# Weight sums made step by step, and the first h quarters loaded into x5's place

## The chip, the cores and the metric

One core of one Trainium2 chip runs the whole program. The metric is the device time of one execution in microseconds (us); the time before is the median of three runs. A profile was taken of one further execution.

## What is computed

One decoder layer on 512 tokens of width 2048, all in float32. Cut to what matters here:

```python
proj = x @ w_in                                        # 2048 -> 4352: q | k | v | B | C | h
attn = sliding_window_gqa(rope(q), rope(k), v, sinks)  # 16 heads of 64, 2 kv heads, window 128
conv = B * causal_depthwise_conv3(C * h)               # 1024 channels
x = layer_norm(ALPHA * x + concat(attn, conv) @ w_out)
u = causal_depthwise_conv3(x @ w_up)                   # 2048 -> 11264
a, g = split(u)
x = layer_norm(ALPHA * x + (silu(a) * g) @ w_down)     # 5632 -> 2048
```

## The kernel before, in words

**Split operands.** TensorE multiplies in fp32r. `split` (L189) cuts a float32 tile into a rounded part (`hi`, a copy on ScalarE, L190) and the rest (`lo`, a subtraction on VectorE, L191), and each product is two or three matmuls (hi by hi, hi by lo, lo by hi).

**Weights.** All weights lie in DRAM as one list `ws` of chunks of 128 x 2048 (1 MB). `dma_to` (L148) loads them in order on SP's queue into `raw` (3 buffers). `split_to` cuts halves of 1024 columns into `whi` and `wlo` (4 buffers each), two halves ahead of the product that uses them.

**The input projection.** `q_panel(0)`: eight halves with 24 matmuls each; here x itself is loaded too (`load_x`, one piece beside each weight chunk) and split. Then four halves for k and v, then eight for the second half of q. `q_evac` applies the rotary factors: two products on VectorE into `wa` and `wb` (two buffers each), and an addition on GpSimd (POOL, L268). Then 48 conv steps (L833 on), each one half of a conv panel in `feat_half` (24 matmuls), with a piece of attention between. Attention begins with `att_q` (L311): a split of q, then transposes on TensorE (L320).

**The output projection and the first normalisation.** `tok_half` steps, again with `half` for the weights; residual rows z are loaded on SP and the gain and bias `gb` on POOL's queue.

**Up product.** Each of 44 column blocks of W_up is done with seven products instead of eight (a Strassen-like scheme). The operands are sums of quarters of x, held in tiles x1 to x7: x1, x2, x4, x7 lie in the four parts of `act`, and x5, x6, x3 in pools of their own. Sums of weight quarters are made by accumulating DMAs on POOL's queue (`w_add`). `product_order` (L58) writes the order out: the last block (43) ends with products 5, 1, (7 and 3 of block 42), 6, 3, (4 of block 42), 7, 2, 4. Results h go to DRAM (`hd`) in groups of four blocks.

**Down product.** Ten column-and-row blocks n, again seven products each, in the order 5, 1, 2, 6, 3, 7, 4. Their h operands are made from quarters of h: `hq_load` (L611) loads four quarters into tiles of the pool `hr`, and `hx` (L617) adds or subtracts on VectorE and splits into a free place from the list `self.free`. Products 5 and 7 need sums of weight quarters that are prepared in DRAM, 20 in all: `w_sum` (L569) copies one chunk from DRAM to DRAM (L577) and then accumulates two half chunks on it (L581), all issued on POOL's queue. Sum 5 of block n is loaded to `wqd` by `d_load` (L583, POOL's queue), sum 7 by `dma_to`.

**What sets the order.** The Tile framework's planner fixes each engine's instruction order from the data dependencies and from its own cost estimates; each engine, and each queue of DMA issues (SP's and POOL's), then executes in that order. An instruction whose inputs and buffer are free may be put far ahead of its place in the source.

The source asks for sums from within the conv loop, one issue step per conv step, and for the h quarters after the last reader of x3:

```python
            self.w_sum(i - 2)                               # conv step i
...
        self.up(20, last)                                   # last = after (43, 3)
        self.d_load(0)
        self.hq_load(0)
```

Of the kernel before, what the change touches and what calls it, by code (L numbers as in the profile page):

```python
# [8 lines left out]
F32 = mybir.dt.float32  # L9
F32R = mybir.dt.float32r  # L10
AF = mybir.ActivationFunctionType
ALU = mybir.AluOpType
AX = mybir.AxisListType

P = 128
S = 512
D = 2048
KT = D // P
# [6 lines left out]
NF = DFF // P  # L25
H = S // 2
# [10 lines left out]
C_OUT = C_CONV + NC_CONV  # L37
# [3 lines left out]
NB = 2 * (NF // 8)  # L41
# [86 lines left out]
class Kernel:  # L128
# [99 lines left out]

    def tok_half(self, j, ks, n, k0, pss, tbs=range(NTB), ahead=2):
        hi, lo = self.half(j, ks, ahead)  # L230
        for k in range(ks):
            kt = k0 + k
            if j == 0 and k == 0:
                ops = ((0, hi), (0, lo), (1, hi))
                for a, (part, ws) in enumerate(ops):
                    for tb in tbs:
                        self.nc.tensor.matmul(pss[tb], self.A(part, 0, slice(tb * P, (tb + 1) * P)), ws[:, 0, :],
                                              start=a == 0, stop=False)
                continue
            for tb in tbs:  # L240
                sl = slice(tb * P, (tb + 1) * P)
                self.mm3(pss[tb][:, :n], self.A(0, kt, sl), self.A(1, kt, sl), hi[:, k, :], lo[:, k, :],
                         kt == 0, kt == KT - 1)
# [322 lines left out]
        c = slice(1024 * h, 1024 * (h + 1))  # L566
        self.nc.gpsimd.dma_start(t[:, c], self.ws_d[C_DOWN + 4 * n + i][:, c], accum_op=ALU.add)

    def w_sum(self, k):  # L569

        s = k // 2 if k % 2 == 0 else (k - 3) // 2
        if not 0 <= s < 2 * NB:
            return
        n, p = s // 2, (5, 7)[s % 2]
        w = lambda i: self.ws_d[C_DOWN + 4 * n + i]
        if k % 2 == 0:
            self.nc.gpsimd.dma_start(self.sums[n, p], w(3))  # L577
        else:
            for h in range(2):
                c = slice(1024 * h, 1024 * (h + 1))  # L580
                self.nc.gpsimd.dma_start(self.sums[n, p][:, c], w(0 if p == 5 else 2)[:, c], accum_op=ALU.add)  # L581

    def d_load(self, n):  # L583

        if n < NB:
            t = self.wq[n] = self.p_qd.tile([P, 2048], F32, name="wqd")
            self.nc.gpsimd.dma_start(t, self.sums[n, 5])

    def down_prep(self, n, p, h):
# [18 lines left out]
        elif h and p in (1, 2, 3, 7):  # L608
            del self.raw[c]

    def hq_load(self, u):  # L611

        for a, t in ((1, 1), (1, 0), (0, 0), (0, 1)):
            tile = self.hq[t, a] = self.p_hr.tile([P, 4, H], F32, name=f"h{t}{a}")
            self.nc.sync.dma_start(tile, self.hd[2 * u + t][:, :, a * H:(a + 1) * H])

    def hx(self, u, p):  # L617

# [129 lines left out]
    def run(self):  # L748
# [28 lines left out]
        ps = self.psum("aux")  # L777
# [56 lines left out]
        for i in range(2 * NC_CONV):  # L834
            j = 2 * C_CONV + i
            q = i % 4
            if q == 0:
                pss = [self.psum("mm") for _ in range(2)]
            hi, lo = self.half(j, 4)
            self.feat_half(hi, lo, q, pss)  # L840
            self.w_sum(i - 2)
            if q == 3:
                self.conv_evac(i // 4, pss)
            for u, off in ((i, 0), (i - 1, 1), (i - 4, 2), (i - 5, 3)):
                if u % 2 == 0 and 0 <= u // 2 < 16:
                    n = u // 2
                    if off == 0:
                        st[n] = self.att_q(*units[n])
                    elif off == 1:
                        st[n] = self.att_scores(*units[n], st[n])  # L850
                    elif off == 2:
                        st[n] = self.att_transpose(*units[n], st[n])
                    else:
                        self.att_values(*units[n], st.pop(n))
# [10 lines left out]
        for k in (slice(0, 2), slice(2, 8)):  # L865
            for tb in range(NTB):
                sl = slice(tb * P, (tb + 1) * P)
                src = self.qm[tb].rearrange("p (k t) -> p k t", t=P)
# [14 lines left out]
        j = 2 * C_OUT  # L883
# [31 lines left out]
        halves = [self.half(j + h, 4, 7 - h) for h in range(4)]  # L915
# [4 lines left out]
        for tb in range(NTB):  # L920
            ps = self.psum("mm")
            sl = slice(tb * P, (tb + 1) * P)
            for kt in range(KT):
                hi, lo = halves[kt // 4]
# [8 lines left out]
        p_x5 = opened("x5", 1, "right")  # L933
        x5 = p_x5.tile([P, KT * H], F32R, name="x5")
# [19 lines left out]
        for tb in (2, 3):  # L954
# [18 lines left out]
        self.up(8, 20)  # L973
        n = len(self.order)
        last = self.order.index((NF - 1, 3)) + 1
        self.up(20, last)
        cm_x3.__exit__(None, None, None)
        cm_x6.__exit__(None, None, None)
        self.p_qd = opened("qd", 2, "right")
        cm_hr, self.p_hr = self.pool("hr", 1, "right")  # L980
        self.hq, self.xd, self.place = {}, {}, {}
        halves = lambda t: [t[:, :KT * P], t[:, KT * P:]]
        self.free = [x for t in (self.act[:, 0, :], x5, self.act[:, 3, :], self.act[:, 1, :], self.act[:, 2, :])
                     for x in halves(t)]
        self.d_load(0)
        self.hq_load(0)
        for i, ps in zip(range(last, n), ((4, 5, 1, 2), (6, 3), (7,), ())):
            self.up(i, i + 1)
            if i == n - 1:
                self.up_conv(NF - 1, 0)  # L990
                self.up_out(NF - 1)
            for p in ps:
                self.hx(0, p)
        for cm, _ in reversed(cm_up):
            cm.__exit__(None, None, None)
        self.z = {}
# [7 lines left out]
        for i, (m, p, h) in enumerate(self.todo[n:]):  # L1004
            self.prepare(n + i + 4)
            u, c = divmod(m, 2)
            ps = self.down_half(m, p, h)
            if not h:
                continue
            self.down_evac(m, p, ps)  # L1010
            if c:
                self.free.append(self.place[u, p])
            if (m, p) == (0, 1):
                self.d_load(1)
            if u + 1 < NB // 2:
                at, q = (1, {3: 4, 7: 5, 4: 1, 11: 2, 12: 6, 16: 3, 13: 7})
                if u == 0:
                    at, q = (3, {4: 4, 11: 5, 12: 1, 16: 2, 13: 6, 17: 3, 14: 7})
                if 10 * c + p == at:
                    self.hq_load(u + 1)  # L1020
                if 10 * c + p in q:
                    self.hx(u + 1, q[10 * c + p])
                continue
            if not c and p == 1:

                places = [self.free.pop(0) for _ in range(2)]
                hs = [x.rearrange("p (f t) -> p f t", f=4) for x in places]
                for t in range(2):
                    raw = self.p_hr.tile([P, 4, H], F32, name=f"h{t}0")
                    tk = slice(t * H, (t + 1) * H)  # L1030
                    nc.sync.dma_start(raw, self.hd[ND - 1][:, :, tk])
                    self.split(hs[0][:, :, tk], hs[1][:, :, tk], raw)
            if (m, p) not in end:
                continue

            k = end.index((m, p))
            if k < 8:
                x1[k] = self.p_hr.tile([P, 4, H], F32, name=("h01", "h11", "h00", "h10")[k % 4])
                x1[k] = x1[k].rearrange("p k t -> p (k t)")
                nc.sync.dma_start(x1[k], zd[k // 2][:, 1024 * (k % 2):1024 * (k % 2 + 1)])  # L1040
            if k >= 2:
                z = self.zc((k - 2) // 2, 1024 * (k % 2), 1024 * (k % 2 + 1))
                nc.vector.scalar_tensor_tensor(z, x1.pop(k - 2), ALPHA, z, op0=ALU.mult, op1=ALU.add)
            if k == 9:
                cm_hr.__exit__(None, None, None)
                p_gb = opened("gb2", 1, "right")
                self.gb = p_gb.tile([P, 2, D], F32, name="gb")
                for a in range(2):
                    nc.gpsimd.dma_start(self.gb[:, a, :], self.lng_d[2 + a].partition_broadcast(P))
# [28 lines left out]
```

## Time and profile before

| what | value |
|---|---|
| runs | 2043.38, 2045.75, 2046.54 us; median 2045.75 |
| the profiled execution | 2044.12 us, of which the span is 2042.3 us |
| mean granted TensorE clock | 0.975 |
| TensorE busy | 1935.0 us (95%) |
| VectorE, ScalarE, POOL busy | 1383.6, 921.3, 308.8 us |
| DMA | 430.19 MB; POOL's queue 174.76 MB, SP's and ScalarE's 252.73 MB |

The span is what lies between the first and the last instruction. In the page's table of 40 slices a slice is 51 us; TensorE's row is below 9 in slices 0, 1 and 3, at the first normalisation (slices 13 and 14), at the change from up to down product (slice 31) and in the last slice. A matmul with 512 columns is shown with 0.39 us, but they overlap: what counts is the distance of their starts.

### The profile page before, as it was taken

What the parts mean: (1) busy time and instruction counts of PE and PEld (TensorE: products, weight loads), DVE (VectorE), ACT (ScalarE), POOL (GpSimd) and SP (SyncE); (2) the same over time, 40 slices, a digit from 0 to 9 for tenths busy, and PEclk for the clock granted to TensorE, in tenths of its full rate; (3) what the DMA queues carried; (4) which work ended last, traced back from release to release, by engine and by line L of the source; (5) the groups of instructions that cost most, each with busy time, mean ns of one, the idle gap of its engine ahead of it and who ended that gap; (6) DMA issues with size and microseconds to landing.
All of it is one profiled execution on the core that took longest, in us unless ns stands there. A gap on an engine that the chain in (4) does not pass through costs nothing. (4 is left out here: it accounts for less than half of the span.)

```text
span 2042.3 us, 26061 instructions
## 1 busy us (share of the span) xinstructions
PE 1935.0 (95%) x9998; PEld 1645.7 (81%) x9998; DVE 1383.6 (68%) x1959; ACT 921.3 (45%) x1403; POOL 308.8 (15%) x361
## 2 busy tenths in 40 slices
PE   7893999999999699999999999999999799999997
PEld 5682888888889588888888888888887588888876
DVE  3332767635334877777777777777777777887887
ACT  2220455433111555555555555555555564454441
POOL 2223000000001511121111111111121001101104
PEclk9896999999999999999999999999999899999999
DMA  9999622154432669999999999999999687877852
GB/s 306 270 295 260 184 78 83 63 165 156 154 103 87 183 155 261 244 261 254 244 262 236 270 254 245 262 242 268 247 249 262 185 235 200 234 225 201 266 193 82
DMA packets 98172, 430.19 MB, mean 211 GB/s; under 512 B 10240, under 2 KB 21536, under 8 KB 72896
## 3 DMA queue, kind: packets, MB, share of 16 engines
q0 software_dynamic: 40928, 174.76, 42.2%
q1 hardware_dynamic: 56544, 252.73, 34.1%
q8 instruction: 78, 1.28, 0.2%
q10 hardware_dynamic: 576, 1.05, 0.1%
q14 instruction: 46, 0.38, 0.1%
HBM read 408.58 MB, written 61.87 MB: 230 GB/s over the span
## 5 line engine op out<-in xcount | busy, mean ns | idle before, releaser
L191 DVE TENSOR_TENSOR wlo<-raw,whi 128x1024 fp32r<-128x1024 f32 (+1 forms) x358 | 437.3, 1223 | 292.8 <-ACT whi L190 292.4
L190 ACT CAST whi<-raw 128x1024 fp32r<-128x1024 f32 (+1 forms) x358 | 373.4, 1045 | 536.3 <-PE mm L222 107.5
L500 PE MATMUL mm<-act,whi 128*128 128x512 f32 x1056 | 379.3, 400 | 8.9 <-DVE act L191 6.7
L502 PE MATMUL mm<-act,wlo 128*128 128x256 f32 x1056 | 297.3, 282 | 0.0
L500 PE MATMUL c<-x,whi 128*128 128x512 f32 x704 | 250.8, 393 | 0.0
L500 PEld LDWEIGHTS mm<-act,whi 128*128 128x128 f32 x1056 | 199.2, 189 | 58.4 <-DVE act L191 7.0
L451 POOL DMA_DIRECT2D wq<-ws x132 | 127.9, 971 | 703.1 <-DVE wlo L191 559.7
L191 DVE TENSOR_TENSOR wlo<-wq,whi 128x1024 fp32r<-128x1024 f32 x132 | 161.3, 1223 | 83.5 <-ACT whi L190 83.3
L502 PEld LDWEIGHTS mm<-act,wlo 128*128 128x128 f32 x1056 | 200.6, 190 | 0.0
L502 PE MATMUL c<-x,wlo 128*128 128x256 f32 x704 | 199.0, 283 | 0.0
L190 ACT CAST whi<-wq 128x1024 fp32r<-128x1024 f32 x132 | 138.5, 1050 | 133.8 <-PE c L500 51.3
L500 PEld LDWEIGHTS c<-x,whi 128*128 128x128 f32 x704 | 132.2, 188 | 30.3
L221 PE MATMUL mm<-act,whi 128*128 128x512 f32 x384 | 152.0, 396 | 0.0
L223 PE MATMUL mm<-act,wlo 128*128 128x512 f32 x384 | 150.4, 392 | 0.0
L222 PE MATMUL mm<-act,whi 128*128 128x512 f32 x384 | 150.1, 391 | 0.0
L221 PE MATMUL mm<-whi,act 128*128 128x512 f32 (+1 forms) x316 | 120.8, 382 | 21.9 <-ACT act L190 20.8
L502 PEld LDWEIGHTS c<-x,wlo 128*128 128x128 f32 x704 | 132.3, 188 | 0.0
L500 PE MATMUL b<-act,whi 128*128 128x512 f32 x352 | 128.5, 404 | 1.5 <-DVE act L191 1.5
L500 PE MATMUL mm<-x,whi 128*128 128x512 f32 x352 | 125.3, 393 | 0.0
L222 PE MATMUL mm<-wlo,act 128*128 128x512 f32 (+1 forms) x316 | 119.6, 378 | 0.3 <-DVE wlo L191 0.3
L223 PE MATMUL mm<-whi,act 128*128 128x512 f32 (+1 forms) x316 | 119.3, 377 | 0.0
L648 PE MATMUL mm<-whi,act 128*128 128x512 f32 x256 | 99.8, 390 | 5.0 <-DVE z L664 3.3
(217 smaller groups left out, 3868.2 us busy)
## 6 DMA issues: line engine op xcount, KB each, us to landing
raw<-ws SPq DMA_DIRECT2D x170, 1024.0 KB, 7.6
wq<-ws POOLq DMA_DIRECT2D x132, 512.0 KB, 9.2
wq<-ws SPq DMA_DIRECT2D x44, 512.0 KB, 8.1
raw<-ws POOLq DMA_DIRECT2D x44, 512.0 KB, 7.2
sum<-ws POOLq DMA_DIRECT2D x40, 512.0 KB, 15.1
wqd<-ws POOLq DMA_DIRECT2D x40, 512.0 KB, 7.2
hd<-ca SPq DMA_DIRECT2D x44, 256.0 KB, 9.6
h<-hd SPq DMA_DIRECT2D x22, 512.0 KB, 5.2
```

The costliest lines, as they stand in the source:

```text
L190: self.nc.scalar.copy(hi, src)
L191: self.nc.vector.tensor_tensor(lo, src, hi.bitcast(F32), op=ALU.subtract)
L221: mm(ps, sh, mh, start=start, stop=False)
L222: mm(ps, sh, ml, start=False, stop=False)
L223: mm(ps, sl, mh, start=False, stop=stop)
L451: self.nc.gpsimd.dma_start(dst, self.ws_d[C_UP + UP_PIECES[2 * f + i]][:, 1024 * j:1024 * (j + 1)], accum_op=ALU.add)
L500: mm(ps, hi[:, sl], x[:, k, :, :].rearrange("p a t -> p (a t)"), start=new and k == 0, stop=False, skip_group_check=not new)
L502: mm(ps[:, :H], lo[:, sl], x[:, k, 0, :], start=False, stop=k == 7, skip_group_check=not new)
L648: mm(ps[b], xh, hi[:, k, :], start=new and h == 0 and k == 0, stop=False, **kw)
```

## The change

Two things are changed. The sums in DRAM: sum s is asked for at conv step 3s, and the last four in the output projection (`tok_half`). A small DMA first copies one element of the step's `wlo` to the sum's place; the chunk copy overwrites it and the accumulations follow, each waiting for the one before. The h quarters: right after product (43, 5), x5's place is taken as a tile of four quarters and `hq_load(0)` loads into it; the operands of the first two blocks go to other places, in another order, and two halves of x5 join the end of the free list. `d_load(1)` is asked for one product earlier, with a ScalarE copy of an element of z (a result of product (0, 5)) into its tile ahead of the load.

```diff
 def tok_half(self, j, ks, n, k0, pss, tbs=range(NTB), ahead=2):
     hi, lo = self.half(j, ks, ahead)
+    if C_OUT <= j // 2:
+        self.w_sum(j - 2 * C_OUT + 48, lo.rearrange("p a b -> p (a b)").bitcast(F32))
...
-def w_sum(self, k):
-    s = k // 2 if k % 2 == 0 else (k - 3) // 2
-    if not 0 <= s < 2 * NB:
+def w_sum(self, k, t):
+    s = k // 3
+    if k % 3 or not 0 <= s < 2 * NB:
         return
     n, p = s // 2, (5, 7)[s % 2]
     w = lambda i: self.ws_d[C_DOWN + 4 * n + i]
-    if k % 2 == 0:
-        self.nc.gpsimd.dma_start(self.sums[n, p], w(3))
-    else:
-        for h in range(2):
-            c = slice(1024 * h, 1024 * (h + 1))
-            self.nc.gpsimd.dma_start(self.sums[n, p][:, c], w(0 if p == 5 else 2)[:, c], accum_op=ALU.add)
+    self.nc.gpsimd.dma_start(self.sums[n, p][0:1, 0:1], t[0:1, 0:1])
+    self.nc.gpsimd.dma_start(self.sums[n, p], w(3))
+    for h in range(2):
+        c = slice(1024 * h, 1024 * (h + 1))
+        self.nc.gpsimd.dma_start(self.sums[n, p][:, c], w(0 if p == 5 else 2)[:, c], accum_op=ALU.add)
-def d_load(self, n):
+def d_load(self, n, after=None):
     if n < NB:
         t = self.wq[n] = self.p_qd.tile([P, 2048], F32, name="wqd")
+        if after is not None:
+            self.nc.scalar.copy(t[:, 0:1], after)
         self.nc.gpsimd.dma_start(t, self.sums[n, 5])
-def hq_load(self, u):
-    for a, t in ((1, 1), (1, 0), (0, 0), (0, 1)):
-        tile = self.hq[t, a] = self.p_hr.tile([P, 4, H], F32, name=f"h{t}{a}")
-        self.nc.sync.dma_start(tile, self.hd[2 * u + t][:, :, a * H:(a + 1) * H])
+def hq_load(self, u, places=None):
+    for q, (a, t) in enumerate(((1, 1), (1, 0), (0, 0), (0, 1))):
+        src = self.hd[2 * u + t][:, :, a * H:(a + 1) * H]
+        ...  # into places[q] where given, else into a tile of hr as before
...
-            self.w_sum(i - 2)
+            self.w_sum(i, lo.rearrange("p a b -> p (a b)").bitcast(F32))
...
     last = self.order.index((NF - 1, 3)) + 1
-    self.up(20, last)
+    k = self.order.index((NF - 1, 5)) + 1
+    self.up(20, k)
+    h0 = p_x5.tile([P, KT * H], F32, name="x5")
+    quarters = h0.rearrange("p (q k t) -> p q k t", q=4, t=H)
+    self.hq_load(0, [quarters[:, q] for q in range(4)])
+    self.up(k, last)
...
-    self.free = [x for t in (self.act[:, 0, :], x5, self.act[:, 3, :], self.act[:, 1, :], self.act[:, 2, :])
+    self.free = [x for t in (self.act[:, 0, :], self.act[:, 3, :], self.act[:, 1, :], self.act[:, 2, :])
                  for x in halves(t)]
     self.d_load(0)
-    self.hq_load(0)
-    for i, ps in zip(range(last, n), ((4, 5, 1, 2), (6, 3), (7,), ())):
+    for i, ps in zip(range(last, n), ((4, 5), (1, 2), (6, 3), (7,))):
         self.up(i, i + 1)
...
+    self.free += halves(p_x5.tile([P, KT * H], F32R, name="x5"))
...
-            if (m, p) == (0, 1):
-                self.d_load(1)
+            if (m, p) == (0, 5):
+                self.d_load(1, self.zc(2, 1024, 1025))
```

## Rows read from the trace of the kernel before

**Rows 1.** Windows: length, busy time (instructions) per engine, granted clock, DMA share, GB/s.

```profile
0.00:84.00 84.00, 60.02 (x200) 43.56 (x201) 25.34 (x35) 21.59 (x30) 16.50 (x32) 0.86 0.97 305
84.00:158.00 74.00, 74.00 (x427) 65.03 (x425) 28.04 (x52) 18.56 (x30) 23.02 (x30) 1.00 0.99 275
158.00:192.00 34.00, 0.79 (x6) 0.57 (x5) 5.88 (x8) 1.04 (x1) 13.44 (x16) 0.53 1.01 257
192.00:496.00 304.00, 304.00 (x1487) 255.00 (x1486) 188.93 (x368) 131.53 (x305) 10.26 (x13) 1.00 0.39 118
...
1580.00:1600.00 20.00, 9.70 (x33) 6.78 (x31) 14.17 (x15) 12.04 (x16) 0.87 (x1) 0.74 0.49 121
1600.00:1620.00 20.00, 15.84 (x57) 12.55 (x58) 16.29 (x17) 9.62 (x13) 1.71 (x2) 0.83 0.88 246
1620.00:1640.00 20.00, 20.00 (x89) 16.52 (x89) 15.31 (x16) 10.26 (x13) 2.27 (x3) 1.00 0.78 218
```

**Rows 2.** Waits, whole run: engine, line, releaser, total us, times, longest us.

```profile
ACT act L190 <- DMA xraw<-xt: 39.6, 9, 10.6
```

**Rows 3.** Groups of TensorE's instructions, 0 to 84 us: busy, mean ns, idle before.

```profile
L221 PE MATMUL mm<-whi,act 128*128 128x512 f32 x60 | 27.6, 461 | 21.9 <-ACT act L190 20.8 <-ACT whi L190 1.1
```

**Rows 4.** Timeline of TensorE: start, duration, line, idle before and releaser.

```profile
6.23 2.07 PE L237 MATMUL mm<-whi,act 128*128 128x512 f32 x4 [0.59 <-ACT whi L190]
...
40.44 0.80 PE L221 MATMUL mm<-whi,act 128*128 128x512 f32 x1 [6.42 <-ACT act L190]
...
191.43 0.75 PE L320 MATMUL aux<-identr,qs 128*128 128x128 f32 x4 [33.21 <-DVE qs L317]
```

**Rows 5.** Timeline of POOL and its DMA issues, 0 to 230 us.

```profile
5.17 1.02 POOL L577 DMA_DIRECT2D sum<-ws  x2
14.14 1.76 POOL L581 DMA_DIRECT2D sum<-ws  x2 [7.96 <-DMA sum<-ws]
...
184.55 2.75 POOL L268 TENSOR_TENSOR qm<-wa,wb 128x512 f32<-128x512 f32 x2
...
220.68 1.64 POOL L581 DMA_DIRECT2D sum<-ws  x2 [8.61 <-DMA sum<-ws]
```

**Rows 6.** Timeline of VectorE, 112 to 200 us.

```profile
186.12 0.69 DVE L263 TENSOR_TENSOR wa<-mm,rope_t 128x512 f32<-128x512 f32 x1 [31.41 <-POOL qm L268]
...
188.65 2.72 DVE L317 TENSOR_TENSOR qs<-qm,qs 128x256 fp32r<-128x256 f32 x1
```

**Rows 7.** VectorE's conv results: count, durations, first and last start.

```profile
L413 DVE TENSOR_TENSOR cmix<-mm,wb x8: 680/688/692, 260.7 to 496.6; 128x512 f32<-128x512 f32 x8
```

**Rows 8.** DMA issues: count, KB each, median us to landing; first 84 to 158 us.

```profile
raw<-ws SPq DMA_DIRECT2D x7, 1024.0 KB, 12.6
...
sum<-ws POOLq DMA_DIRECT2D x40, 512.0 KB, 15.1
out<-z SPq DMA_DIRECT2D x14, 256.0 KB, 2.2
sum<-ws POOLq DMA_DIRECT2D x20, 18.3
```

**Rows 9.** Waits of TensorE, 1570 to 1700 us.

```profile
PE mm L500 <- DVE mt L508: 2.1, 1, 2.1
```

**Rows 10.** Timelines of TensorE, POOL, SP and ScalarE around the change to the down product.

```profile
1552.65 0.28 PE L502 MATMUL c<-x,wlo 128*128 128x256 f32 x1
...
1564.50 1.09 POOL L587 DMA_DIRECT2D wqd<-sum  x2 [6.82 <-PE mm L502]
...
1567.08 8.46 SPq L615 DMA_DIRECT2D h<-hd  x4
...
1573.06 1.05 ACT L190 CAST whi<-wqd 128x1024 fp32r<-128x1024 f32 x1 [4.76 <-DMA wqd<-sum]
...
1584.72 1.04 ACT L190 CAST x<-h 128x1024 fp32r<-128x1024 f32 x1 [3.07 <-DMA h<-hd]
...
1588.60 1.04 ACT L190 CAST x<-h 128x1024 fp32r<-128x1024 f32 x1 [1.89 <-DMA h<-hd]
```

More of the change, by code (lines that the diff above doesn't have):

```diff
@@ L609, in down_prep @@
             del self.raw[c]
-    def hq_load(self, u):
-        for a, t in ((1, 1), (1, 0), (0, 0), (0, 1)):
-            tile = self.hq[t, a] = self.p_hr.tile([P, 4, H], F32, name=f"h{t}{a}")
-            self.nc.sync.dma_start(tile, self.hd[2 * u + t][:, :, a * H:(a + 1) * H])
+    def hq_load(self, u, places=None):
+        for q, (a, t) in enumerate(((1, 1), (1, 0), (0, 0), (0, 1))):
+            src = self.hd[2 * u + t][:, :, a * H:(a + 1) * H]
+            if places is None:
+                tile = self.p_hr.tile([P, 4, H], F32, name=f"h{t}{a}")
+                self.nc.sync.dma_start(tile, src)
+            else:
+                tile = places[q]
+                self.nc.sync.dma_start(tile, src)
+            self.hq[t, a] = tile
     def hx(self, u, p):
@@ L975, in run @@
         last = self.order.index((NF - 1, 3)) + 1
-        self.up(20, last)
+        self.hq, self.xd, self.place = {}, {}, {}
+        k = self.order.index((NF - 1, 5)) + 1
[4 more added lines that the diff above has]
+        self.up(k, last)
         cm_x3.__exit__(None, None, None)
@@ L980, in run @@
         cm_hr, self.p_hr = self.pool("hr", 1, "right")
-        self.hq, self.xd, self.place = {}, {}, {}
         halves = lambda t: [t[:, :KT * P], t[:, KT * P:]]
-        self.free = [x for t in (self.act[:, 0, :], x5, self.act[:, 3, :], self.act[:, 1, :], self.act[:, 2, :])
+        self.free = [x for t in (self.act[:, 0, :], self.act[:, 3, :], self.act[:, 1, :], self.act[:, 2, :])
                      for x in halves(t)]
         self.d_load(0)
-        self.hq_load(0)
-        for i, ps in zip(range(last, n), ((4, 5, 1, 2), (6, 3), (7,), ())):
+        for i, ps in zip(range(last, n), ((4, 5), (1, 2), (6, 3), (7,))):
             self.up(i, i + 1)
```

## The prediction

> **What bounds the kernel now.** I read the page's 40 slices first (TensorE below 9 tenths in few of them), then windows cut at those slices, then the waits of each low window, then the timelines. TensorE is the bound wherever its inputs are there: 74.00 of 74 us busy from 84 to 158 us, 304.00 of 304 through the conv stage [rows 1]. So a gain can only come from its idle stretches, and those touched by the change are three.
>
> The first is the first panel, 0 to 84 us: TensorE waits 20.8 us for x's split [rows 3], ScalarE in turn 39.6 us for x from DRAM [rows 2], while the DMA engines are 97% busy [rows 1]. What fills them are the sums, written in the conv loop but issued from 5.17 us on [rows 5], since nothing holds them back.
>
> The second is the gap of 33.2 us ahead of the first attention transposes [rows 4]. Its chain: TensorE waits for VectorE's split of q, which stands in VectorE's order behind the rotary products; those waited 31.4 us for their buffer [rows 6], which POOL's rotary addition frees; that addition ran at 184.55 us because POOL's queue was standing in the accumulations, each waiting for its copy to land [rows 5].
>
> The third is the change to the down product, 1580 to 1620 us: ScalarE waits for the h quarters, the third and fourth of four, split at 1584.72 and 1588.60 us [rows 10]; the reader is to see that they were issued at 1567.08 us, though x5 had its last reader at 1552.65 us.
>
> **The change, part by part.**
>
> *First panel.* It has 192 matmuls (three groups of 60, of which one is shown [rows 3], and 12 started apart). At full clock 89 take 20 us [rows 1], 0.225 us each, so 43.2 us. The 12 at the start, of which four take 2.07 us [rows 4], cost some 2.5 us more and keep that. From 6.2 us the panel could end at 52 us instead of 84: 32 us lost, made of idle time and of the low clock (mean 0.86 [rows 1]) after each gap. With no sums the loads move only weights and x, 8.4 MB for those 46 us, 183 GB/s; the DMA engines moved 305 GB/s there [rows 1]. A lower end: some gaps at the start, when everything lands at once, stay (7 us). I keep 1.5 us: gain 30.5, range 25 to 32.
>
> *The gap at the conv stage.* The accumulations leave POOL's queue ahead of the rotary additions, except those of sum 0: its marker waits for the split of the first conv half, which is made two halves ahead, thus while q's last panel still runs. Behind the marker stands the copy, behind it the accumulations, and if the planner puts these ahead of the additions, the additions wait for the copy's landing; VectorE's rotary products and the q split wait for them. The first copies landed within 14.14 - 5.17 = 9.0 us, beside other loads [rows 5]; VectorE stood ready for its third rotary product at 186.12 - 31.41 = 154.7 us [rows 6], 3.5 us before TensorE ran out at 191.43 - 33.21 = 158.2 [rows 4], so the additions were due before that. Thus between 0 and 9 us of the 33.2 stay. From the additions to the transposes it was 191.43 - 184.55 = 6.9 us [rows 4, 5], which alone leaves 1 to 2. I take 1.7: gain 31.5, range 24 to 34 (the upper end with the low clock after the gap).
>
> *Where the sums go.* Conv steps take (496.6 - 260.7) / 36 = 6.55 us [rows 7], so a sum comes every 19 us or so and the last fall into the output projection. Moved there: 20 copies and 40 accumulations, plus 20 markers. DMA was 39% busy in the conv stage, its first 38 us still with sums [rows 1]. Cover: the weights are loaded three chunks ahead, and a chunk lasts two steps, 13 us. With sums running without pause a chunk landed in 12.6 us [rows 8], and TensorE missed nothing in that stretch although it used a chunk in about 11 us [rows 1]. So I cost this at 0, bound 0 to 15 us, should the loads be late now and then. A marker reads `wlo`, whose buffer is wanted again four steps (26 us) later. No marker is in the trace; the nearest row, a store of 256 KB, lands in 2.2 us [rows 8], a chunk copy in 18.3 at worst of load. Hidden, 0; below nothing it can't go, as it does no work of before.
>
> *The h quarters.* In 1580 to 1620 us TensorE did 33 + 57 = 90 matmuls, for which it needs 20.2 us at the rate of the window after [rows 1]. Lost 19.8 us, and 2.1 us in a wait just ahead [rows 9]: 21.9 us. Now the four loads can start when product (43, 5) ends at 1552.65, 14.4 us sooner than 1567.08 [rows 10]. On SP's queue they wait for that product; behind them stand stores of h and raw chunks for the down product, which take their turn once it ends. The four took 21.5 us to the last split (1567.08 to 1588.60 [rows 10]) in company of 2 MB of `wqd` and other loads; so all are there by 1574 at the latest, before the last up product ends. d_load(1), which was issued along with d_load(0) at 1564.50 [rows 10], is held back until product (0, 5) is out, which leaves its 1 MB some five products of 5.4 us (24 matmuls) to land in. Its ScalarE copy is one element a row: nothing.
>
> What is late next: VectorE. It was busy 14.17 + 16.29 = 30.5 us in those 40 [rows 1]; if TensorE is to pass through in 20 us, what of this is not done earlier must fit beside it. Only products 4 and 5's operands can move ahead of 1570; products 1, 2, 6, 3 and 7 now take places (x7's, x2's, x4's) that come free with the last three up products, later than x5's half, which served 1 and 2 before. And `wqd` for product (0, 5) still comes at 1573 [rows 10] unless fewer loads run beside it. I keep 6 of the 21.9: gain 16, range -3 (a chain put in a worse order) to 21.
>
> *Sum.* 30.5 + 31.5 + 0 + 16 = 78 us. Everything after each gap is TensorE-bound, so the shifts carry through. The profiled execution took 2044.1 us (its span 2042.3 and 1.8 around it); 2044.1 - 78 = 1966.1. The median is 1.6 above that execution: 1968 us.
>
> **Rivals.**
>
> *The sums hurt where they now run* (slower). If each sum delayed TensorE as it did in the first panel, where some seven sums cost 32 us, 20 sums cost 91 us: 2044 - 78 + 91 + 2 = 2059 us. It decides once a chunk takes over some 25 us to land, twice its use. For it: the first panel itself. Against it: the first panel needed x besides, 1 MB in 5.4 us, twice the conv stage's need or more, and the stretch from 84 to 158 us ran full under the same load [rows 1]. The Trainium skill, in "DMA: Bandwidth & Descriptors", section "Issuing engines are not separate DMA queues", says that DMAs started from different engines run on the same 16 DMA engines and interleave; by that alone the collisions would only move. Trace and rule agree on the collision, in the first panel.
>
> *The marker chain paces TensorE.* Copy and accumulations in series, each as late as before: 2.2 + 18.3 + 15.1 = 35.6 us [rows 8] a sum instead of 19, with `wlo` held: 20 x 16.6 - 26 = 306 us, 2274 us in all. Against it: those landings come from several sums at once; one alone needs the 9 us of the first copies and about as much again, and POOL doesn't wait for the accumulations' end.
>
> *The h part gives nothing.* The planner may put the second set of h loads, which no longer waits for the first's tiles, as far ahead as d_load(1) was, so that they collide with `wqd`; or VectorE stays the limit. Then 1984 us.
>
> *Only half of the conv gap goes*: sum 0's accumulations stand before the additions, and what they delay is a chain of several engines: 15 of 33 us stay, 1981 us.
>
> *The change doesn't do what it says*: the sums' order is still the planner's. But the marker is a data dependency on a split, so no sum can start before it; I give this little. With the first panel alone improved: about 2014 us.
>
> **How the numbers follow.** The forecast as worked out 0.66 (1955 to 1978); h part nothing 0.13; conv gap half 0.08; both of these or the doing-less case 0.05 (1990 to 2020); sums hurt in the conv stage 0.05, of which half ends above the time before; marker chain 0.03. What a measurement can tell from no change is 0.2%, 4 us. Faster: the first four and half of the fifth, 0.94; within 4 us: 0.01; slower: 0.05. Best ends give 2044.1 - 32 - 34 - 21 + 1.6 = 1959; some unlisted gain of the shift may come on top, so low 1954. The high end takes in the two smaller cases: 1995.
>
> **What would show it.** After: first copy on POOL's queue past 100 us; the first panel's end near 53 us with no wait over 2 us; POOL's additions right behind VectorE's products and the transposes' wait under 3 us; raw chunks landing in under 13 us in the conv stage and TensorE full there; h loads issued some 14 us before the last product that reads x3 ends; TensorE's clock at 1.00 through the change to the down product, or else waits there for VectorE. Wrong would be the sum if TensorE shows new waits for `wlo` or raw in the conv stage, or if the additions still stand behind a landing.

## The result, and the profile after

The changed kernel takes 1969.53 us (median of 4 runs, 1967.84 to 1970.89); the kernel before took 2045.31 beside it. The ratio is 0.963, with a 95% interval of 0.9613 to 0.9647. The profiled execution has a span of 1969.1 us, 73.2 less than before, and a mean granted clock of 0.989 against 0.975. The forecast was 1968.

The windows of the changed kernel, cut at the same stages; the columns are those of [rows 1]:

```profile
0.00:52.00 52.00, 50.09 (x203) 38.99 (x204) 25.61 (x36) 21.67 (x30) 5.02 (x16) 1.00 0.65 255
52.00:126.00 74.00, 74.00 (x430) 65.19 (x429) 30.41 (x59) 19.02 (x31) 16.51 (x16) 1.00 0.37 114
126.00:430.00 304.00, 304.00 (x1492) 255.02 (x1492) 190.95 (x370) 132.83 (x306) 45.36 (x65) 1.00 0.74 202
...
1510.00:1520.00 10.00, 8.72 (x35) 7.36 (x36) 9.41 (x14) 8.20 (x13) 1.71 (x2) 0.83 0.90 219
1520.00:1530.00 10.00, 5.00 (x23) 3.79 (x21) 9.99 (x12) 8.13 (x11) 0.56 (x1) 0.97 0.48 151
1530.00:1540.00 10.00, 9.63 (x30) 7.75 (x31) 9.20 (x9) 4.13 (x5) 1.71 (x2) 0.68 0.86 271
```

The reader is to see three things. The first panel, 84 us with a clock of 0.86 before, is done in 52 with a clock of 1.00. No window stands between the end of q, k and v and the conv stage: the 34 us of 158 to 192 are gone. And the conv stage is as full as it was (304.00 of 304), although DMA is now busy for 74% of it and not 39%. At the change to the down product, though, TensorE still loses time, and VectorE is busy 9.2 to 10 us of each 10.

ScalarE's wait for x in the first panel, which was 39.6 us [rows 2], and the loads of x on SP's queue, first of the kernel before, then of the changed one (count, KB each, median us to landing):

```profile
ACT act L190 <- DMA xraw<-xt: 5.0, 6, 2.2
```

```profile
xraw<-xt SPq DMA_DIRECT2D x6, 512.0 KB, 32.4
...
xraw<-xt SPq DMA_DIRECT2D x6, 512.0 KB, 9.6
```

POOL and TensorE where the gap was (timelines; compare [rows 5] and the last row of [rows 4]):

```profile
105.03 0.54 POOL L579 DMA_DIRECT2D sum<-wlo  x1 [24.24 <-DVE wlo L191]
106.92 0.51 POOL L580 DMA_DIRECT2D sum<-ws  x1 [1.34 <-DMA sum<-wlo]
112.16 1.75 POOL L583 DMA_DIRECT2D sum<-ws  x2 [4.74 <-DMA sum<-ws]
119.31 2.56 POOL L270 TENSOR_TENSOR qm<-wa,wb 128x512 f32<-128x512 f32 x2 [5.40 <-DVE wb L268]
```

```profile
125.57 0.45 PE L322 MATMUL aux<-identr,qs 128*128 128x128 f32 x4
```

Sum 0 is begun at 105 us, its two accumulations leave the queue together from 112.16 us on (each waits for the copy, neither for the other), and the rotary additions, at 119.31, wait for VectorE's product and not for a landing. The transposes follow without a wait where 33.2 us stood.

In the conv stage, VectorE's results and the DMA issues of 130 to 430 us (issues: KB each, median us to landing):

```profile
L415 DVE TENSOR_TENSOR cmix<-mm,wb x8: 682/691/692, 193.5 to 429.3; 128x512 f32<-128x512 f32 x8
```

```profile
raw<-ws SPq DMA_DIRECT2D x23, 1024.0 KB, 5.1
sum<-ws POOLq DMA_DIRECT2D x30, 512.0 KB, 8.5
...
sum<-ws POOLq DMA_DIRECT2D x16, 5.1
sum<-wlo POOLq DMA_DIRECT2D x15, 0.0 KB, 4.8
```

The first and the last result come 67.2 us earlier than in [rows 7], so all of this part of the gain is there before the conv stage and nothing is lost in it. A chunk of weights lands in 5.1 us where the sums ran beside it in 12.6 before [rows 8].

The waits of TensorE at the change to the down product, and the timeline there, all engines in one by their start:

```profile
PE mm L660 <- DVE wlo L191: 5.4, 1, 5.4
PE mm L502 <- DVE mt L510: 2.8, 1, 2.8
```

```profile
1485.61 0.28 PE L504 MATMUL c<-x,wlo 128*128 128x256 f32 x1
...
1485.98 4.65 SPq L625 DMA_DIRECT2D x<-hd  x4
...
1497.47 0.55 POOL L592 DMA_DIRECT2D wqd<-sum  x1 [6.45 <-PE mm L504]
...
1507.22 1.05 ACT L190 CAST whi<-wqd 128x1024 fp32r<-128x1024 f32 x1 [4.98 <-DMA wqd<-sum]
...
1522.54 1.22 DVE L630 TENSOR_TENSOR x<-x 128x1024 f32<-128x1024 f32 x1
...
1527.36 1.22 DVE L191 TENSOR_TENSOR act<-x,act 128x1024 fp32r<-128x1024 f32 x1
...
1529.10 3.49 DVE L191 TENSOR_TENSOR wlo<-raw,whi 128x1024 fp32r<-128x1024 f32 x3
...
1530.37 0.79 PE L660 MATMUL mm<-wlo,act 128*128 128x512 f32 x1 [5.38 <-DVE wlo L191]
```

The h loads leave 0.4 us after the last matmul of product (43, 5) starts (14.4 before [rows 10]). But the weight split that TensorE wants at 1525 stands on VectorE behind sums and splits of h operands (the L630 and act rows) that are only needed later.

### The profile page after: what moved, and what is told of

The parts are those of the page before. It is cut to its first block, busy times and chain, and to the rows that moved or that the text cites. A ratio compares the mean times of both kernels' runs of the same rounds, so it can differ in the third digit from the quotient of the medians.

```text
span 1969.1 us, 26106 instructions
## 1 busy us (share of the span) xinstructions
PE 1923.1 (98%) x9998; PEld 1640.4 (83%) x9998; DVE 1380.6 (70%) x1959; ACT 920.8 (47%) x1404; POOL 323.0 (16%) x381
## 5 line engine op out<-in xcount | busy, mean ns | idle before, releaser
L221 PE MATMUL mm<-whi,act 128*128 128x512 f32 (+1 forms) x316 | 116.5, 369 | 0.0
L223 PE MATMUL mm<-whi,act 128*128 128x512 f32 (+1 forms) x316 | 116.2, 368 | 0.0
L660 PE MATMUL mm<-wlo,act 128*128 128x512 f32 x272 | 107.4, 395 | 5.4 <-DVE wlo L191 5.4
```

Source lines behind the costliest of these rows:

```text
L221: mm(ps, sh, mh, start=start, stop=False)
L223: mm(ps, sl, mh, start=False, stop=stop)
L660: mm(ps[b], xh, lo[:, k, :], start=False, stop=False, **kw)
```

## The experiments

**One half at a time.** `sums_only` keeps the sums' part and undoes the h part; `h_only` does the opposite:

```diff
 # sums_only, against the changed kernel
-    h0 = p_x5.tile(...); self.hq_load(0, [quarters[:, q] for q in range(4)])
...
+    self.hq_load(0)                 # after d_load(0); operand order, places, d_load(1) as before
 # h_only: w_sum as before
-    self.nc.gpsimd.dma_start(self.sums[n, p][0:1, 0:1], t[0:1, 0:1])
...
+    self.w_sum(i - 2)
```

> Only the sums are paced by markers; the h quarters and the places are as before. Theory (the sums' part is worth the 67 us by which every stage after the conv gap is earlier in the changed kernel): 2045.3 - 67 = 1978 us, span shift 67 at the end of the up product and still 67 at the end, with the stalls at the change to the down product as before (16.6 us of waits). Rival (the two parts need each other, or part of the 67 belongs to the h part): over 1985 us.

> Only the h quarters' part (early loads into x5's place, other places, d_load(1) held); the sums are asked for as before. Theory from the traces (the h part gains 9.6 us up to product (0, 3) of the down product, and some 3 us are lost again in the last stage): 2045.3 - 6.5 = 2039 us. The prediction's term was 16: 2029 us. Rival (the h part gains nothing by itself): within 4 us of 2045.

`sums_only` took 1976.76 us, ratio 0.9651 (0.9633 to 0.9668), span 1975.0: 67.3 less than before. `h_only` took 2038.05, ratio 0.9945 (0.993 to 0.996): 11.1 less than the 2049.19 of before beside it (8 to 14 by the interval; 6.1 in the spans, 2042.3 - 2036.2). Both came within 1.3 us of their theories. Nearly everything is the sums' part, and the h part is worth less than the 16 us forecast: 11.1 alone, and in the spans 1975.0 - 1969.1 = 5.9 on top of the other (1975.0 - 1966.9 = 8.1 with the second profile of the changed kernel, below). By the ratios 0.9651 and 0.9630, or 0.9620 in the repeat, it is 4 to 6 us, uncertain by some 5.

**The two gaps of the sums' part.** `sums_after_panel` is the kernel before with 20 small copies, one per sum, tied to the third weight half of k and v, so that the sums start only after the first panel, and are unpaced from there on. `rope_vector` is the kernel before with the rotary additions on VectorE:

```diff
 # sums_after_panel, in q_panel
+        if j == 10:
+            self.marks(lo)     # sums[n, p][0:1, 0:1] <- lo[0:1, 0:1], for all 20
 # rope_vector
-        nc.gpsimd.tensor_tensor(dst, t1, t2, op=ALU.add)
+        nc.vector.tensor_tensor(dst, t1, t2, op=ALU.add)
```

> The kernel before with 20 markers alone, all tied to the third k and v half, so that the sums start at the end of the first panel and then run without pause, on POOL's queue ahead of the rotary additions as before. Theory (two separate causes: DMA contention in the first panel, and POOL's order at the conv gap): the first panel's 32 us go, the conv gap of about 33 us stays: 2013 us. If contention alone made both, the gap would go or change with the load: rival 1980 to 1990 us.

> The kernel before with one edit: the rotary additions (12 instructions) run on VectorE instead of POOL; the sums start at 5 us as before. Theory (the gap of 33 us is POOL's order, not a lack of data): the wait ahead of the first attention transposes falls from 33.2 to under 5 us and the first panel stays at 84 us: 2045.3 - 30 = 2015 us. Rival (the gap is the loads' lateness, with POOL only last by chance): raw chunks or kv data take its place, gain under 10 us, over 2035 us.

`sums_after_panel` took 2007.38 us, ratio 0.9798 (0.9782 to 0.9813). Its first panel ends at 50 us, and the gap stays. POOL's timeline, then TensorE's:

```profile
136.94 1.64 POOL L583 DMA_DIRECT2D sum<-ws  x2 [5.86 <-DMA sum<-ws]
...
146.93 0.81 POOL L583 DMA_DIRECT2D sum<-ws  x1 [7.84 <-DMA sum<-ws]
147.49 1.54 POOL L270 TENSOR_TENSOR qm<-wa,wb 128x512 f32<-128x512 f32 x1
```

```profile
152.65 0.75 PE L322 MATMUL aux<-identr,qs 128*128 128x128 f32 x4 [28.85 <-DVE qs L319]
```

The addition starts as soon as an accumulation has left the queue ahead of it, which itself waited 7.84 us for a copy. `rope_vector` took 2009.49, ratio 0.9806 (0.9791 to 0.982), with the sums as early as before. Its transposes don't wait, and its first panel does (timeline and waits of TensorE):

```profile
158.80 0.45 PE L320 MATMUL aux<-identr,qs 128*128 128x128 f32 x4
```

```profile
PE mm L221 <- ACT act L190: 17.7, 5, 5.3
```

Each removes one gap and leaves the other, and each is worth some 40 us against the median of 2049.19 beside them, or 37.7 and 34.2 us in the spans, against 2042.3. Both theories, 2013 and 2015 us, were some 6 us too slow, and the two gains don't quite add up: together they are more than the 72.4 of `sums_only` beside the same runs. In `sums_after_panel` the gap is 28.85 us and not 33.2, which is part of it. The rivals lay 17 us and more away. So the chain is shown: the sums' traffic starves the first panel, and the sums' waits on POOL's queue hold the rotary additions. The Trainium skill ("DMA: Bandwidth & Descriptors", section "Issuing engines are not separate DMA queues") says that transfers of all queues share the 16 engines; the first panel agrees (97% busy, [rows 1], and x, loaded on SP's queue, lands in 32.4 us with POOL's sums beside it and in 9.6 without). The second gap is no matter of bandwidth at all: the same DMA traffic, with the additions on another engine, left no wait.

**Does the pacing matter, or only the start?** `one_marker` is the changed kernel with all 20 small copies tied to conv step 4 and nothing between the sums after that:

```diff
-            self.w_sum(i, lo.rearrange("p a b -> p (a b)").bitcast(F32))
+            if i == 4:
+                self.marks(lo)
+            self.w_sum(i - 6)   # copy, or two accumulations, as before the change
```

> The changed kernel, but with its sums held only at one point: 20 small copies tied to the split of conv step 4, after which nothing paces them (a copy or a pair of accumulations asked for per conv step, issued as fast as POOL's queue lets them). Theory (what mattered is only that the sums are out of the first panel and behind the rotary additions; TensorE has room for them anywhere in the conv stage): 1967 to 1973 us, within 0.2% of the changed kernel's 1969.0; TensorE full from the conv stage's begin to its end, DMA share near 1.0 in its first 150 us or so, raw chunks landing in 11 to 14 us there. Rival (the step by step pacing is worth something itself): the weight chunks come late while the sums run unpaced, TensorE waits for whi or wlo in the conv stage, 1979 us or more. Second rival: the sums are done earlier and the output projection has less to move, so 1965 us or less.

It took 1968.28 us, ratio 0.9619 (0.9605 to 0.9633): as the changed kernel. Its windows, and its DMA issues of 126 to 300 us:

```profile
126.00:200.00 74.00, 74.00 (x370) 62.20 (x369) 50.02 (x106) 32.34 (x83) 24.00 (x40) 1.00 0.94 259
200.00:250.00 50.00, 50.00 (x260) 42.23 (x259) 33.18 (x71) 25.66 (x66) 10.87 (x15) 1.00 1.03 291
250.00:300.00 50.00, 50.00 (x260) 42.20 (x259) 35.36 (x76) 24.19 (x64) 10.79 (x15) 1.00 1.02 280
```

```profile
raw<-ws SPq DMA_DIRECT2D x13, 1024.0 KB, 11.3
```

DMA is busy for 0.94 to 1.03 of its time for 174 us, weights land in 11.3 us (median) and not 5.1, and TensorE misses nothing. That the sums are spread "step by step" is worth nothing here; that they begin after the first panel, and after the rotary additions of q, is worth all of it.

**The h part: order on VectorE.** `hx_late` asks for the operands of products 3 and 7 of the first block after its products 5 and 1 (x5's halves join the free list behind them). It ran with a repeat of the changed kernel (`after_again`):

```diff
-    for i, ps in zip(range(last, n), ((4, 5), (1, 2), (6, 3), (7,))):
+    for i, ps in zip(range(last, n), ((4, 5), (1, 2), (6,), ())):
...
+            if (m, p) == (0, 5):
+                self.hx(0, 3)
+            if (m, p) == (0, 1):
+                self.hx(0, 7)
```

> The changed kernel itself, as the measure for the others of this job: 1969 us if the median of before is about 2045, in the same ratio (0.963) if it is higher.

> The changed kernel; the operands of products 3 and 7 (two additions and two splits on VectorE, 4.9 us) are asked for after products (0, 5) and (0, 1) instead of before the first down product. Theory (what keeps the h part from its 16 us is VectorE's order: 9.99 us busy of 10, three weight splits behind those operands, TensorE 5.4 us waiting for wlo, then the low clock): that wait falls under 1 us, 5 to 9 us faster than the changed kernel. Rival (VectorE has too much work in any order): the wait moves to products 6 and 3, gain under 2 us.

`after_again` took 1969.02 us, ratio 0.962 (0.9607 to 0.9633); `hx_late` 1961.43 (1957.61 to 1962.91), ratio 0.9581 (0.9567 to 0.9596), span 1958.5 against 1966.9. It beats both kernels. Its windows and TensorE's waits there:

```profile
1510.00:1520.00 10.00, 10.00 (x48) 8.19 (x48) 10.00 (x13) 9.11 (x13) 1.43 (x3) 1.00 0.98 220
1520.00:1530.00 10.00, 9.37 (x41) 7.09 (x40) 9.29 (x12) 6.70 (x9) 0.61 (x1) 1.00 0.80 266
```

```profile
PE mm L502 <- DVE mt L510: 1.7, 1, 1.7
...
PE b L660 <- DVE wlo L191: 0.4, 1, 0.4
PE mm L660 <- DVE wlo L191: 0.2, 1, 0.2
```

VectorE does the same work, in another order; the wait for `wlo` goes from 5.5 to 0.6 us and the clock stays at 1.00. So most of what the h part still lost was VectorE's order and the low clock after it.

**The wait of 2.5 us for `mt`** (2.8 in the first profile of the changed kernel). ScalarE, and behind it VectorE, stand in the landing of the weight sum `wqd` while an evacuation of the last up products is due. `wqd_cast_pool` puts the rounding copies of product (0, 5)'s weights on POOL, `hold_h1` holds the second set of h loads (which the planner moved up to 1500 us) until product (0, 5) is out, and `late_pool_split` is `hx_late` with both the copies and the subtractions on POOL:

```diff
 # wqd_cast_pool, in down_prep, for (n, p) == (0, 5); late_pool_split: both on gpsimd
-        self.split(hi, lo, src[:, cs])
+        self.nc.gpsimd.tensor_copy(hi, src[:, cs])
+        self.nc.vector.tensor_tensor(lo, src[:, cs], hi.bitcast(F32), op=ALU.subtract)
 # hold_h1, in hq_load, for the second set
+                self.nc.scalar.copy(tile[:, 0, 0:1], after)   # after = an element of z
```

> The changed kernel; the two casts of the first down weights (wqd of product (0, 5)) run on POOL instead of ScalarE. Theory (the wait of 2.8 us ahead of product (43, 4) comes of ScalarE standing 5.0 us in this cast for wqd's landing, with an evacuation behind it): the 2.8 us and the low clock after it go, 3 to 5 us faster than the changed kernel. Rival (the evacuation waits for something else, or POOL's slower cast delays product (0, 5) by as much): within 1.5 us of it, or slower.

> The changed kernel; the second set of h quarters, issued at 1500 to 1506 us there, is held by a ScalarE copy of a result of product (0, 5), as d_load(1) is. Rival cause of the 2.8 us wait named in the prediction (the second h loads collide with wqd): wqd lands 2 to 4 us sooner and the wait halves, 2 to 4 us faster. Theory against it (wqd shares the engines with two raw chunks anyway): under 1 us.

> The changed kernel with the operands of products 3 and 7 asked for after products 5 and 1 (as hx_late, 1961.4 us), and the whole split of product (0, 5)'s weight sum (rounding copy and subtraction) on POOL in place of ScalarE and VectorE. Theory (with neither engine standing in the landing of the sum's load, the evacuations of the last up products are not held up): the wait of 1.7 us of a matmul for VectorE's mt goes, all waits at the change to the down product together under 1 us, 1958 to 1961 us. Rival (POOL's split of 4 x 1024 columns is too slow and comes later than product (0, 5) wants it): a new wait of TensorE for POOL's wlo of 2 us or more, 1963 us or more. Rival (the matmul waits for something else than the engine's stand): wait unchanged at 1.7 us, same time as hx_late within 1 us.

`wqd_cast_pool` took 1968.59 us, ratio 0.9619 (0.9606 to 0.9632), and its wait is 2.2 us: the theory fell, and the time is that of the changed kernel. VectorE stands in the same landing, with the subtraction:

```profile
1505.88 2.03 DVE L606 TENSOR_TENSOR wlo<-wqd,whi 128x1024 fp32r<-128x1024 f32 x1 [1.79 <-POOL whi L605]
...
1508.49 0.41 DVE L510 TENSOR_TENSOR mt<-mm,mt 128x256 f32<-128x256 f32 x1
```

`hold_h1` took 1972.51, ratio 0.9639 (0.9626 to 0.9653), no gain: it is 3.5 us above `after_again`, with intervals that overlap, and its wait for `wlo` is 7.0 us and not 5.5. Its window shows that the loads were held:

```profile
1500.00:1510.00 10.00, 8.10 (x46) 6.75 (x45) 7.05 (x11) 5.24 (x9) 0.19 (x1) 1.00 0.67 276
```

The DMA share there is 0.67, where the changed kernel has 1.00, but `wqd` landed no sooner after its issue (cast 9.3 us after it, against 9.4 in `after_again`), and the wait stayed at 2.3. So the second set of h loads is not what makes `wqd` late; what does isn't settled.

`late_pool_split` took 1964.12 (1961.25 to 1965.46), ratio 0.9597 (0.9582 to 0.9611), not faster than `hx_late`. The wait for `mt` is gone as the theory had it, and the time came back elsewhere, so that the first rival had the time right (1963 us or more) but not the wait: TensorE waits 0.7 us for POOL's `wlo` and 3.4 us for a later one of VectorE's, mainly because VectorE became slower while POOL split (the planner also put the split of an operand, 1.2 us, ahead of it). POOL's timeline, then VectorE's, then VectorE's in `hx_late` for the same operation:

```profile
1509.92 1.32 POOL L605 CAST whi<-wqd 128x1024 fp32r<-128x1024 f32 x1
1511.32 2.46 POOL L606 TENSOR_TENSOR wlo<-wqd,whi 128x1024 fp32r<-128x1024 f32 x1
```

```profile
1509.48 2.04 DVE L510 TENSOR_TENSOR ug<-m,mt 128x256 f32<-128x256 f32 x1
1511.45 4.54 DVE L191 TENSOR_TENSOR act<-x,act 128x1024 fp32r<-128x1024 f32 x2
```

```profile
1510.30 0.42 DVE L510 TENSOR_TENSOR ug<-m,mt 128x256 f32<-128x256 f32 x1
1510.64 2.35 DVE L191 TENSOR_TENSOR act<-x,act 128x1024 fp32r<-128x1024 f32 x2
```

An instruction of 0.42 us took 2.04 and a pair of 2.35 us took 4.54, each beside one of POOL's. The Trainium skill ("SBUF — State Buffer", section "Who interferes with whom") says that a VectorE operation with two inputs from SBUF and a GpSimd operation that reads SBUF exclude each other for a whole instruction; the rows agree: VectorE's pair ends at 1511.45 + 4.54 = 1515.99, 2.2 us after POOL's end at 1511.32 + 2.46 = 1513.78, about its own length of 2.35. The instruction of 0.42 us fits less well: it ends 0.3 us after POOL's cast, but starts 0.4 us before it (starts and lengths on POOL are rough).

## Why the prediction was right, and where it was not

*First panel: right in mechanism, 2 us short.* The first matmul of k comes at 51.97 us, where it came at 84.47: 32.5 us, against 30.5 with a range to 32. The load was sized too small: the DMA engines moved 255 GB/s in those 52 us, 13.3 MB, and not 8.4 MB at 183 GB/s, since 8 MB of weights were loaded and not 4. At a DMA share of 0.65 this did no harm. ScalarE's wait for x from DRAM is 5.0 us in all, where it was 39.6 [rows 2]. The 1.5 us kept for remaining gaps were not needed: TensorE waits once for `whi`, 0.7 us. `sums_after_panel` shows this part by itself.

*The gap at the conv stage: right in mechanism, 3 us short.* Of the shift of 67.2 us behind it [rows 7], 67.2 - 32.5 = 34.7 come from here: the 33.2 us and some 1.5 of slow matmuls after it. Forecast were 31.5, with a range to 34. The 1.7 us left for the way from the addition to the transposes were not lost, since TensorE had other matmuls until 125.57; and sum 0's accumulations were out 5 us before the additions were due (112.16 + 1.75 against 119.31), so that the case of only half a gain didn't come up. `rope_vector` shows the mechanism: POOL's order, not bandwidth.

*Sums where they now run: right.* 0 us. `one_marker` shows how much room there is. The marker rival had a trace of truth: from 390 to 520 us markers, issued right behind accumulations, land only after 9.4 to 13.7 us, and VectorE waited 16.5 us in two waits for a `wlo` that a marker still read. TensorE had no wait there. The 18.3 us that the prediction takes for a copy "at worst of load" are the median of all 20 [rows 8]; the rival was sized with it, the forecast of 0 was not.

*The h quarters: the term that was mis-sized.* The step "I keep 6 of the 21.9: gain 16" failed. From the end of product (43, 5) to the first c matmul of product (0, 3) it took 1545.94 - 1485.61 = 60.3 us, before 1622.56 - 1552.65 = 69.9: a gain of 9.6 (that c matmul before, in the changed kernel, and in `hx_late`):

```profile
1622.56 0.39 PE L648 MATMUL c<-whi,act 128*128 128x512 f32 x1
...
1545.94 0.39 PE L659 MATMUL c<-whi,act 128*128 128x512 f32 x1
...
1535.85 0.39 PE L659 MATMUL c<-whi,act 128*128 128x512 f32 x1
```

Nine up products of 2.82 us and four down products of 5.46 need 47.2, so 13 us stayed lost and not 6: the waits of 5.4 and 2.8, and some 4.9 behind them, most of it low clock (matmuls 0.43 us apart and not 0.23, at the lower of the clock's two levels, 1.2 and not 2.4 GHz; 0.83 and 0.68 are the means of the windows). The prediction named VectorE as what is late next, but sized it by its busy time and not by its order: operands of products 3 and 7 ahead of the weight split for the product that is due. `hx_late`, which changes this order alone, takes 8.4 us off the span (against `after_again`) and leaves 2.3 us of waits. From the end of product (43, 5) to the same matmul it needs 1535.85 - 1485.21 = 50.6 us, 19.3 less than before: the 16 were there to be had. The loads themselves came as forecast, and the second set did move up as the rival said, without harm (`hold_h1`).

*What came on top.* Just ahead of the last stage's one wait the shift was 76.6 us, at the end of the span 73.2. The last stage is 3.4 us slower. The wait itself is 0.5 us longer (3.3 before), and 1.5 us are the clock after it, in the changed kernel and in `sums_only`:

```profile
1905.29 0.76 PE L659 MATMUL mm<-whi,act 128*128 128x512 f32 x1 [3.78 <-DVE z L675]
```

```profile
1913.86 0.47 PE L659 MATMUL mm<-whi,act 128*128 128x512 f32 x1 [3.66 <-DVE z L675]
```

After much the same wait the first runs its next matmuls 0.43 us apart and the second 0.23. It would be easy to blame the new places for the h operands, since seven of the eight profiles with them show the slow start. But `hold_h1` has them and starts at full clock, and `rope_vector`, with the places of before, ran slow from its third matmul on (the matmul behind the wait in `hold_h1`, then the third behind it in `rope_vector`):

```profile
1904.61 0.47 PE L661 MATMUL mm<-whi,act 128*128 128x512 f32 x1 [3.73 <-DVE z L677]
```

```profile
1946.19 0.63 PE L650 MATMUL mm<-whi,act 128*128 128x512 f32 x1
```

The granted clock is 0.66 from 1905 to 1910 us in the changed kernel and from 1945 to 1950 in `rope_vector`, and 1.00 from 1904 to 1909 in `hold_h1`. So the places don't decide it, and what does is not shown. Then a block of 48 matmuls takes 11.15 us and not 10.97, four times, 0.7 us in all; this is so in all eight profiles with the new places and in none of the four others, but why was not tried. The last 0.8 us lie behind the last matmul, in the last normalisation, which takes 11.4 to 12.3 us with the old places as with the new.

So the total came near partly by luck, by errors of both signs: in the spans the sums' part gave 67 where 62 were forecast, and the h part 6 (9.6 less 3.4) where 16 were, together 73 for 78. Between the medians it is 2045.75 - 1969.53 = 76.2, since the one profiled execution was a little below its median and the other above.

## What to carry to other kernels

A DMA with nothing to wait for is issued as early as the planner and the queue let it: give it a data dependency on the point where its bandwidth is free, and one such point was enough here (`one_marker`). A DMA that waits for another DMA held up all that its issuing engine had behind it (33.2 us by way of POOL's additions), so look at that engine's compute, not only at the DMA share. When loads come earlier, the next limit can be the order of the engine that prepares them, as VectorE's was here: size it by what stands ahead of the work that is due, not by its busy share.

## What was not expected of the hardware

With the DMA engines at 1.02 to 1.03 of their time for 100 us (`one_marker`), weights of 1 MB still landed in 11.3 us, and a full TensorE noticed nothing; much the same load in the first panel (0.97), where x was wanted as well, cost 32 us. And work moved from VectorE to POOL was not work taken off VectorE (`late_pool_split`): a subtraction of 1.22 us went, and the pair of instructions beside it on VectorE took 4.54 - 2.35 = 2.2 us longer.
